# Turning the first chunk of the normed x at the layer change by VectorE blocks and DRAM

## The chip, the cores and the metric

The kernel runs on one core of one Trainium2 chip. The metric is the device time of one execution in microseconds (us). The time before is the median of three runs.

## The reference

Two layers of a decoder trunk over 512 tokens of width 1024. Each layer norms x, projects it once, feeds four groups of heads, gates them, projects back, norms again and adds to x:

```python
def hybrid_layer(x, mem, pre_g, post_g, w_in, ..., mem_norm_g, w_mem_kv, w_out):
    hn = rmsnorm(x, pre_g)
    proj = hn @ w_in                       # 1024 -> 6664 columns
    (ret_q, ..., xbc, z, dt_raw, sb_q, sb_k, sb_v, sb_g, mem_q, mem_g) = jnp.split(proj, ...)
    y_ret = retention(...) * silu(ret_g)
    y_ssd = ssd_mixer(xbc, z, dt_raw, ...)
    y_sb = stick_breaking(sb_q, sb_k, sb_v) * silu(sb_g)
    y_mem = memory_read(mem_q, rmsnorm(mem, mem_norm_g), w_mem_kv) * silu(mem_g)
    y = jnp.concatenate([y_ret, y_ssd, y_sb, y_mem], axis=-1) @ w_out
    return x + rmsnorm(y, post_g)          # x of the next layer
```

All is float32. What matters here is the seam between layer 0 and layer 1: `x + rmsnorm(y, post_g)`, then `rmsnorm(x, pre_g)` of the next layer, then the first products `hn @ w_in`, for which hn has to lie with its features on the partitions.

## The kernel before

The tokens are cut into four chunks of 128 (t = 0 to 3, `NT`). Matmuls in full precision are three products of two halves: `split` writes a high part (fp32r, a CAST on ScalarE, L293) and the remainder (a subtraction on VectorE, L294), and `mm3` (its matmuls all stand at L285) multiplies high by high, high by low and low by high. The normed x is kept turned, features first, as `hTh` (high) and `hTl` (low), each 128 partitions by 8 feature blocks by 512 tokens. Weights stream in through ScalarE's DMA queue (L353) as `raw`, and are split into `wh` and `wl` (five buffers each). PSUM has four banks named `pj` and four named `mx`. SBUF work tiles come from slots `s` (33), `y` (16) and `r` (9).

The layer change lies in `out_proj`. The second half of the output projection runs the four chunks two steps apart, so their sums end one after the other. For each chunk `post` then takes the square sums (ScalarE, L1168), a reciprocal root on GpSimd (L449 and L450), the new x on VectorE (L1170, two of L1172), two stores of it to DRAM for the end of layer 1 (SP's queue, L1179), the norm for layer 1 (two squares on ScalarE, L462; GpSimd again; two products on VectorE, L470, each 128x512), and turns the result. `turned` (through `prenorm`) turns 128x512 twice: four TensorE transposes of 128x128 into one `mx` bank (L479), then `split` from the bank into `hTh` and `hTl`.

While that goes on, TensorE does work of layer 1 that does not need x: the keys of the memory (`mem_k`, called twice, 256 columns wide) and its values (`mem_v`). `behind` ties the place of a transpose to these: the turn of chunk 0 stands behind the last matmul of the first `mem_k`, that of chunk 1 behind the second, that of chunk 2 behind a late matmul of `mem_v`, and that of chunk 3 (in `sb_v`) behind one in the first products with x. The first reader of `hTh` is `sb_v`'s `proj_a` (264 columns: 256 of a value block and 8 of the time steps); it runs chunk by chunk, chunk 0 first. Its banks are `pj` banks that `mem_k2` empties (VectorE, L570).

Apart from these ties, a scheduler with a model of time sets the order on each engine. Each engine then works strictly in that order, waiting on semaphores; SP's queue too.

The kernel already has another way to turn a tile, for the attention weights: VectorE's transpose turns each 32x32 block in place of the whole, four DMAs write the four groups of 32 partitions so that the blocks land in turned places of a DRAM tile, and one DMA reads the tile back (`through_dram`, L645 to L652: writes at L650, read at L651):

```python
        for a in range(P // BLK):
            self.nc.sync.dma_start(dst[a], v3(T[BLK * a:BLK * a + BLK], n))
        self.nc.sync.dma_start(out, src)
```

The functions that the diff touches:

Of the kernel before, what the change touches and what calls it, by code (L numbers as in the profile page):

```python
# [8 lines left out]
F32 = mybir.dt.float32  # L9
# [7 lines left out]
P = 128  # L17
SEQ = 512
NT = SEQ // P
D = 1024  # L20
KC = D // P
# [132 lines left out]

BLK = 32
TT = "y"
ST, SL, SB1, SB2 = "s", "y", 2, 4
# [11 lines left out]
def v3(ap, a):  # L171
    return ap.rearrange("p (a b) -> p a b", a=a)


class Builder:
# [305 lines left out]
            out(4 * i, b)  # L481
        return first

    def prenorm(self, x, gB, t):
        return self.turned(self.normed(x, gB), t)

    def turned(self, hn, t):
        ts = slice(P * t, P * t + P)
# [141 lines left out]
    def mem_turn(self, h, w, y):  # L630
        nc = self.nc
        pT = []
        for m in range(2):
            T = self.buf(tag="y")
            for i in range(2):
                x = w[i].rearrange("p (t m j b) -> p m t j b", t=2, m=2, b=BLK)[:, m]
                nc.vector.transpose(T.rearrange("p (j t b) -> p t j b", t=NT, b=BLK)[:, 2 * i:2 * i + 2], x)
            d = self.turned_rows(P, SEQ)
            dd = d.rearrange("(j m) (a t) -> a m j t", m=BLK, a=P // BLK)
            pT.append(self.through_dram(T, dd, d, self.buf(tag="y")))  # L640
# [5 lines left out]
    def through_dram(self, T, dst, src, out):  # L646

        n = dst.shape[2]
# [3 lines that stand above are left out]
        return out  # L652

    def columns_turned(self, tiles, out):
# [3 lines left out]
        for k, x in enumerate(tiles):  # L658
            T = self.buf(n, TT)
            self.nc.vector.transpose(T, x)  # L660
            dd = d[:, P * k:P * k + P].rearrange("(b t) (a f) -> a t b f", t=BLK, a=P // BLK)
            for a in range(P // BLK):
# [433 lines left out]
    def y_pair(self, kc):  # L1096
        return self.pair(self.yT[OUT_KEYS[kc]])

    def out_proj(self, l):
        nc = self.nc  # L1100
        last = l == DEPTH - 1
        y_pair, ys, ys2 = self.y_pair, self.ys, {}
        self.turn = []
        banks = [self.pj() for _ in range(NT)]
        for kc in range(16):
            if 1 <= kc < 15:
                ys[kc + 1] = y_pair(kc + 1)
            elif kc == 15:
                ys2 = {0: y_pair(0), 1: y_pair(1)}
            if kc % 2 == 0:  # L1110
                self.tick()
                w = self.w_take(2)
            for t in range(NT):
                self.out_unit(banks[t], ys[kc], kc, t, w)
            if kc % 2:
                self.w_prefetch()
            if kc == 6 and not last:
                self.mem_load()
            if kc == 8 and not last:
                self.mem_tiles()  # L1120
                for i in range(4):
                    self.mem_pairs(l + 1, i)
        postB = self.bcast_row(self.a["post_norm_g"][l:l + 1])
        preB = None if last else self.bcast_row(self.a["pre_norm_g"][l + 1:l + 2])
        y0 = [self.buf() for _ in range(NT)]
        ss = [self.tiny(2) for _ in range(NT)]
        for t in range(NT):
            nc.vector.tensor_tensor(out=y0[t], in0=banks[t], in1=postB[0], op=ALU.mult)
            nc.scalar.activation(banks[t], banks[t], AF.Square, scale=1.0 / 32.0, accum_out=ss[t][:, 0:1])
            self.with_eps(ss[t][:, 0:1])  # L1130
        banks = [self.mx() for _ in range(NT)]
        ys, subs, x1 = ys2, {}, []
        for step in range(16 + self.SKEW * (NT - 1)):
            if step == 8:
                xs = [self.load_x(t) for t in range(NT)]
            if 2 <= step + 1 < 16:
                ys[step + 1] = y_pair(step + 1)
            for t in range(NT):
                kc = step - self.SKEW * t
                if not 0 <= kc < 16:  # L1140
                    continue
                if kc // 2 not in subs:
                    subs[kc // 2] = self.w_take(2)
                self.out_unit(banks[t], ys[kc], kc, t, subs[kc // 2])
                if t == NT - 1 and kc % 2:
                    self.w_prefetch()
                if kc == 15:
                    x1.append(self.post(l, t, xs[t], y0[t], banks[t], ss[t], postB[1], preB))
        self.yT = {}
        self.xsrc = x1  # L1150
        if not last:
            for i in range(2):
                self.mem_k2(self.mem_k(i))
                self.behind(self.turn[i], self.last_mm)
            self.mem_v()
            self.behind(self.turn[2], self.marks[5])

    def load_x(self, t):
        x = [self.buf(), self.buf()]
# [4 lines left out]
    def post(self, l, t, x, y0, bank, ss, g1, preB):  # L1164

        nc = self.nc
        y1, junk = self.buf(), self.buf()
        nc.scalar.activation(junk, bank, AF.Square, scale=1.0 / 32.0, accum_out=ss[:, 1:2])  # L1168
        r = self.rstd(ss[:, 0:1], ss[:, 1:2])
        nc.vector.tensor_tensor(out=y1, in0=bank, in1=g1, op=ALU.mult)  # L1170
        for i, y in enumerate((y0, y1)):
            nc.vector.scalar_tensor_tensor(out=x[i], in0=y, scalar=r, in1=x[i], op0=ALU.mult, op1=ALU.add)  # L1172
        if preB:
            d = self.dr.tile([P, D], F32, tag="x1", name=self.name("x1"), bufs=NT)[:]
            self.turn.append(self.prenorm(x, preB, t))
        else:
            d = self.a["out"][P * t:P * t + P]
        for i in range(2):
            nc.sync.dma_start(d[:, 512 * i:512 * i + 512], x[i])  # L1179
        return d  # L1180
# [154 lines left out]
```

## Time and profile before

| | |
|---|---|
| median of 3 runs | 922.68 us (922.54 to 923.47) |
| profiled execution | 923.25 us, its span 921.5 us |
| granted TensorE clock over the span | 0.998 |
| busy: TensorE, VectorE, ScalarE, GpSimd | 99%, 73%, 48%, 16% of the span |
| layer change (first L1168 to first reads of hTh) | 461 to 488 us of the span |

The span is what the profiler saw from the first to the last instruction; 1.75 us of the execution lie around it. Places in the span are given in us from its start. In a row of the timeline, the first number is the start, the second the length of the merged piece, and a bracket at the end tells idle time before it and what ended that. TensorE's matmuls overlap in such rows, so the distance from one start to the next, not the length, is what one of them takes. PE is TensorE, PEld its weight load, DVE VectorE, ACT ScalarE, POOL GpSimd, SP the queue of SyncE; a q behind the name is the engine's instruction queue.

### The profile page before, as it was taken

The page shows a single profiled execution, that of the slowest core. Times are in us where ns is not written, and L with a number is a line of the kernel's source. Part 1 is how long each engine was busy: PE and PEld are TensorE (multiplying, and loading weights), DVE is VectorE, ACT ScalarE, POOL GpSimd, SP SyncE. Part 2 cuts the span into 40 slices and gives each one's busy share as a digit, 9 for nine tenths or more (in the row PEclk, how much of TensorE's full clock was granted, in tenths as well). Part 3 has the DMA queues.
Part 4 walks back from the last instruction along what each step waited for, and adds up shares of the span by engine and source line. Part 5 has one row for each costly group of instructions (what it writes and reads, how often), then busy time and mean ns, then how long its engine had stood idle before and what let it go on. Part 6 is the DMA issues. An engine that isn't in the chain of part 4 may idle for free.

```text
span 921.5 us, 12952 instructions
## 1 busy us (share of the span) xinstructions
PE 913.2 (99%) x4667; PEld 773.6 (84%) x4667; DVE 673.3 (73%) x1081; ACT 443.5 (48%) x841; POOL 146.3 (16%) x208
## 2 busy tenths in 40 slices
PE   9999999999999999999999999999999999999997
PEld 7998888888888888888899888888888888888885
DVE  6855689888787887844587476898778869687343
ACT  6643485744453342733465336675445434335341
POOL 1200152320131110100040002423112120102001
PEclk9999999999999999999999999999999999999999
DMA  8544664642444333444345256556333362422502
GB/s 316 213 141 144 169 167 104 199 146 61 120 134 148 116 109 126 137 149 158 116 173 196 93 172 183 124 122 183 103 109 116 110 194 92 139 95 88 210 12 91
DMA packets 105408, 128.53 MB, mean 139 GB/s; under 512 B 64640, under 2 KB 79744, under 8 KB 96256
## 3 DMA queue, kind: packets, MB, share of 16 engines
q10 hardware_dynamic: 10224, 73.44, 23.4%
q1 hardware_dynamic: 95120, 54.28, 20.7%
q8 instruction: 36, 0.59, 0.3%
q14 instruction: 28, 0.23, 0.1%
HBM read 112.10 MB, written 15.56 MB: 139 GB/s over the span
## 4 chain that ended last, share of the span: by engine, by line
PE 98%; DMA 1%; ACT 0%; DVEq 0%; SPq 0%; POOLq 0%; issue 0%; POOL 0%; ACTq 0%; DVE 0%
PE pj L285 74%; PE mx L285 23%; PE mx L479 1%; DMA mem<-memT 1%; PE mx L1003 0%; ACT s L523 0%; DVEq L1331 0%; ACT s L1168 0%; POOLq L1331 0%; ACT wh L293 0%; SPq L506 0%; SPq L349 0%; SPq L1206 0%; POOL t L449 0%; ACTq L1331 0%
## 5 line engine op out<-in xcount | busy, mean ns | idle before, releaser
L285 PE MATMUL pj<-hTh,wh 128*128 128x512 f32 x704 | 276.4, 393 | 0.0
L285 PE MATMUL pj<-hTh,wl 128*128 128x512 f32 x704 | 275.8, 392 | 0.0
L285 PE MATMUL pj<-hTl,wh 128*128 128x512 f32 x704 | 274.6, 390 | 0.0
L294 DVE TENSOR_TENSOR wl<-raw,wh 128x1024 fp32r<-128x1024 f32 (+2 forms) x156 | 188.6, 1214 | 116.9 <-ACT wh L293 115.7
L293 ACT CAST wh<-raw 128x1024 fp32r<-128x1024 f32 (+2 forms) x156 | 158.7, 1020 | 205.0 <-PE pj L285 177.5
L285 PEld LDWEIGHTS pj<-hTh,wl 128*128 128x128 f32 x704 | 132.2, 188 | 27.3
L285 PEld LDWEIGHTS pj<-hTh,wh 128*128 128x128 f32 x704 | 132.3, 188 | 27.1 <-DVE s L593 0.8
L285 PEld LDWEIGHTS pj<-hTl,wh 128*128 128x128 f32 x704 | 132.3, 188 | 26.6
L285 PE MATMUL pj<-wh,s 128*128 128x512 f32 x320 | 97.6, 391 | 0.0
L285 PE MATMUL mx<-s,s 128*128 128x256 f32 (+4 forms) x528 | 79.7, 307 | 0.0
L285 PE MATMUL mx<-wh,s 128*128 128x512 f32 x256 | 79.2, 389 | 0.0
L285 PEld LDWEIGHTS mx<-s,s 128*128 128x128 f32 (+1 forms) x528 | 65.8, 177 | 8.2 <-PE pj L285 1.4
L285 PEld LDWEIGHTS pj<-wh,s 128*128 128x128 f32 x320 | 59.7, 188 | 12.4
L285 PE MATMUL pj<-wl,s 128*128 128x512 f32 x160 | 60.2, 389 | 0.0
L285 PEld LDWEIGHTS mx<-wh,s 128*128 128x128 f32 x256 | 48.1, 188 | 10.0
L294 DVE TENSOR_TENSOR s<-y,s 128x512 fp32r<-128x512 f32 x64 | 41.2, 687 | 19.7 <-ACT s L293 14.0
L262 ACT ACTIVATE s<-s 128x128 f32<-128x128 f32 (+3 forms) x96 | 41.8, 478 | 22.3 <-DVE s L733 20.6
L675 POOL TENSOR_TENSOR s<-y,s 128x512 fp32r<-128x512 f32 x16 | 23.7, 1494 | 179.9 <-ACT s L674 179.4
L293 ACT CAST s<-y 128x512 fp32r<-128x512 f32 x64 | 36.6, 617 | 30.8 <-PE mx L285 22.0
L285 PE MATMUL mx<-wl,s 128*128 128x512 f32 x128 | 49.6, 389 | 0.0
L285 PE MATMUL pj<-wl,hTh 128*128 128x256 f32 (+2 forms) x144 | 47.6, 331 | 0.0
L285 PE MATMUL pj<-wh,hTl 128*128 128x256 f32 (+2 forms) x144 | 47.5, 330 | 0.0
(185 smaller groups left out, 1298.5 us busy)
## 6 DMA issues: line engine op xcount, KB each, us to landing
raw<-wts ACTq DMA_DIRECT2D x69, 1024.0 KB, 4.8
s<-x SPq DMA_DIRECT2D x24, 256.0 KB, 4.1
y<-turned SPq DMA_DIRECT2D x24, 256.0 KB, 2.8
turned<-y SPq DMA_DIRECT2D x64, 64.0 KB, 2.2
s<-acs SPq DMA_DIRECT2D x16, 256.0 KB, 6.3
r<-row SPq DMA_DIRECT2D x12, 256.0 KB, 5.0
raw<-wts SPq DMA_DIRECT2D x4, 512.0 KB, 7.5
raw<-wts SPq DMA_DIRECT2D x2, 1024.0 KB, 6.3
```

The source lines that it names most:

```text
L262: i = self.nc.scalar.activation(out, in_, func, **k)
L285: return self.nc.tensor.matmul(out, lhsT, rhs, start=start, stop=stop)
L293: self.nc.scalar.copy(h, src)
L294: self.nc.vector.tensor_sub(l, src, hf)
L479: x = self.nc.tensor.transpose(b[:, P * j:P * j + P], hn[i][:, P * j:P * j + P], self.con("ident", P))
L675: nc.gpsimd.tensor_sub(p.l, x, p.hf)
```

## The change

For chunk 0 alone (`FAR` = 1) the eight TensorE transposes go. Each of the two 128x512 halves of the normed x is turned by one VectorE transpose into a `y` slot, written to a DRAM tile of 512x128 by four DMAs of 64 KB (runs of 128 bytes), read back by one DMA of 256 KB (runs of 512 bytes) into another `y` slot, and split from there. Chunks 1 to 3 are turned as before. The tie of chunk 0's transposes to `mem_k` goes with them; the other ties stay.

```diff
+LT, LL, FAR = "y", "y", 1
...
-    def prenorm(self, x, gB, t):
-        return self.turned(self.normed(x, gB), t)
+    def turned_far(self, hn, t):
+        ts = slice(P * t, P * t + P)
+        H, HF, L = v3(self.hTh[:], KC), v3(self.hTh[:].bitcast(F32), KC), v3(self.hTl[:], KC)
+        for i in range(2):
+            T, ks = self.buf(tag=LT), slice(4 * i, 4 * i + 4)
+            self.nc.vector.transpose(T, hn[i])
+            d = self.turned_rows(SEQ, P)
+            dd = d.rearrange("(b m) (a t) -> a m b t", m=BLK, a=P // BLK)
+            x = self.through_dram(T, dd, d.rearrange("(k p) t -> p k t", p=P), v3(self.buf(tag=LL), 4))
+            self.split(x, H[:, ks, ts], L[:, ks, ts], HF[:, ks, ts])
...
                 self.mem_k2(self.mem_k(i))
-                self.behind(self.turn[i], self.last_mm)
+                if i >= FAR:
+                    self.behind(self.turn[i], self.last_mm)
...
-            self.turn.append(self.prenorm(x, preB, t))
+            self.turn.append((self.turned_far if t < FAR else self.turned)(self.normed(x, preB), t))
```

The scheduler orders the seam anew. GpSimd's order is the same as before, and on the other engines nothing changes outside the layer change and the first few projections of layer 1. In the rows below a name carries a running number, which differs between the two programs; after the change a line stands 1 to 12 lines further down (L479 is L480, L470 is L471, L1172 is L1184, L293 and L294 are L294 and L295).

VectorE at the norm of chunk 0 and what follows it. Before: s_4544 and s_4545 are the normed halves of chunk 1, hTl from mx_4492 and mx_4499 is chunk 0, s_4332 and s_4333 are the new x of chunk 2.

```order
L294 TENSOR_TENSOR wl_4694<-raw_4376,wh_4693 128x1024
L294 TENSOR_TENSOR wl_4724<-raw_4450,wh_4723 128x1024
L1170 TENSOR_TENSOR s_4585<-mx_4214,s_4185 128x512
L470 SCALAR_TENSOR_TENSOR s_4544<-s_4328,t_4549,s_4188 128x512
L470 SCALAR_TENSOR_TENSOR s_4545<-s_4329,t_4549,s_4189 128x512
L294 TENSOR_TENSOR hTl<-mx_4492,hTh 128x4x128
L1172 SCALAR_TENSOR_TENSOR s_4332<-s_4194,t_4588,s_4332 128x512
L294 TENSOR_TENSOR hTl<-mx_4499,hTh 128x4x128
L1172 SCALAR_TENSOR_TENSOR s_4333<-s_4585,t_4588,s_4333 128x512
L294 TENSOR_TENSOR wl_4759<-raw_4450,wh_4758 128x1024
L294 TENSOR_TENSOR wl_4789<-raw_4697,wh_4788 128x528
```

The same place after (y_4492 and y_4503 are the block-turned halves of chunk 0, y_4495 the first half read back):

```order
L295 TENSOR_TENSOR wl_4702<-raw_4376,wh_4701 128x1024
L491 STREAM_TRANSPOSE y_4492<-s_4482 128x512
L295 TENSOR_TENSOR wl_4732<-raw_4450,wh_4731 128x1024
L1182 TENSOR_TENSOR s_4593<-mx_4214,s_4185 128x512
L471 SCALAR_TENSOR_TENSOR s_4552<-s_4328,t_4557,s_4188 128x512
L471 SCALAR_TENSOR_TENSOR s_4553<-s_4329,t_4557,s_4189 128x512
L1184 SCALAR_TENSOR_TENSOR s_4332<-s_4194,t_4596,s_4332 128x512
L295 TENSOR_TENSOR wl_4767<-raw_4450,wh_4766 128x1024
L1184 SCALAR_TENSOR_TENSOR s_4333<-s_4593,t_4596,s_4333 128x512
L295 TENSOR_TENSOR wl_4797<-raw_4705,wh_4796 128x528
L491 STREAM_TRANSPOSE y_4503<-s_4483 128x512
L295 TENSOR_TENSOR hTl<-y_4495,hTh 128x4x128
```

One transpose stands behind the first of two weight splits, the other eight instructions later; chunk 0's first low half moves from ahead of chunk 2's new x to behind it, and its second low half, 12 rows further on, stands just ahead of chunk 3's norm.

ScalarE between the squares of chunk 2 and the third block of 264 columns' weights. Before (s_4596 and s_4597 are the squares of chunk 2, s_4632 the square sum of chunk 3, hTh from mx_4554 and mx_4561 is chunk 1):

```order
L293 CAST wh_4788<-raw_4697 128x528
L462 ACTIVATE s_4596,t_4595<-s_4332 128x512
L462 ACTIVATE s_4597,t_4595<-s_4333 128x512
L1168 ACTIVATE s_4632,t_4199<-mx_4215 128x512
L293 CAST hTh<-mx_4554 128x4x128
L353 DMA raw_4762<-wts 128x1056
L293 CAST hTh<-mx_4561 128x4x128
L293 CAST wh_4848<-raw_4697 128x528
L462 ACTIVATE s_4642,t_4641<-s_4336 128x512
L462 ACTIVATE s_4643,t_4641<-s_4337 128x512
L293 CAST wh_4854<-raw_4762 128x528
```

After (hTh from y_4495 and y_4506 are the two halves of chunk 0 as they come back from DRAM):

```order
L463 ACTIVATE s_4604,t_4603<-s_4332 128x512
L354 DMA raw_4770<-wts 128x1056
L294 CAST hTh<-y_4495 128x4x128
L463 ACTIVATE s_4605,t_4603<-s_4333 128x512
L1180 ACTIVATE s_4640,t_4199<-mx_4215 128x512
L294 CAST hTh<-mx_4562 128x4x128
L294 CAST hTh<-mx_4569 128x4x128
L294 CAST wh_4856<-raw_4705 128x528
L463 ACTIVATE s_4650,t_4649<-s_4336 128x512
L294 CAST wh_4862<-raw_4770 128x528
L463 ACTIVATE s_4651,t_4649<-s_4337 128x512
L294 CAST hTh<-y_4506 128x4x128
```

The cast of the first half now stands between the two squares of chunk 2, that of the second behind the squares of chunk 3.

TensorE at the first reads of hTh. Before, pj_4877 (chunk 0) takes twelve matmuls, and then pj_4878 (chunk 1):

```order
L285 MATMUL pj_4877<-wh_4848,hTh 128x264
L285 MATMUL pj_4877<-wl_4849,hTh 128x264
L285 MATMUL pj_4877<-wh_4848,hTl 128x264
L285 MATMUL pj_4878<-wh_4788,hTh 128x264
L285 MATMUL pj_4878<-wl_4789,hTh 128x264
```

After, with pj_4885 for chunk 0, pj_4886 for chunk 1 and wh_4862 the first weights of the second half of the features:

```order
L286 MATMUL pj_4885<-wl_4857,hTh 128x264
L286 MATMUL pj_4885<-wh_4856,hTl 128x264
L286 MATMUL pj_4885<-wh_4862,hTh 128x264
L286 MATMUL pj_4886<-wh_4796,hTh 128x264
L286 MATMUL pj_4886<-wl_4797,hTh 128x264
```

Chunk 0's first half of features is read by the 1st matmul of this block as before, the second half's high part by the 13th, and its low part by the 27th. Before, chunk 0's transposes stood as two groups of four in the second `mem_k`; there is nothing in their place now, and chunk 1's two groups of four have become one of eight, 20 matmuls into `mem_v`.

SP's queue gets ten DMAs: four writes and a read behind the two stores of chunk 1's x, and four writes and a read behind the two stores of chunk 2's x. The stores of chunk 3's x stand behind all of these.

More of the change, by code (lines that the diff above doesn't have):

```diff
@@ L1153, in out_proj @@
                 self.mem_k2(self.mem_k(i))
-                self.behind(self.turn[i], self.last_mm)
+                if i >= FAR:
+                    self.behind(self.turn[i], self.last_mm)
             self.mem_v()
-            self.behind(self.turn[2], self.marks[5])
+            if FAR < 3:
+                self.behind(self.turn[2], self.marks[5])
     def load_x(self, t):
```

## The prediction

> **What bounds the kernel now.** First the busy times and the chain that ended last, from the page, and the waits of TensorE over the whole run.
>
> ```profile
> PE 913.2 (99%) x4667; PEld 773.6 (84%) x4667; DVE 673.3 (73%) x1081; ACT 443.5 (48%) x841; POOL 146.3 (16%) x208
> PE 98%; DMA 1%; ACT 0%; DVEq 0%; SPq 0%; POOLq 0%; issue 0%; POOL 0%; ACTq 0%; DVE 0%
> PE mx L285 <- POOL b L197: 1.2, 1, 1.2
> PE pj L285 <- ACT s L523: 1.0, 2, 0.7
> ```
>
> TensorE is busy for all but 8 us, the chain is TensorE for 98%, and its only two waits belong to the start (L197 is the warm-up, L523 the first memory tiles). From then on it never waits, so what is taken off it comes off the end, as long as no new wait appears. Next the seam itself, engine by engine (columns: length, PE, PEld, DVE, ACT, POOL busy with counts, granted clock, DMA share, GB/s).
>
> ```profile
> 455.00:475.00 20.00, 20.00 (x139) 18.61 (x138) 15.75 (x20) 11.72 (x23) 6.84 (x12) 1.00 0.53 186
> 475.00:488.00 13.00, 13.00 (x68) 10.85 (x68) 12.56 (x20) 8.95 (x21) 4.92 (x8) 1.00 0.51 185
> 488.00:515.00 27.00, 27.00 (x216) 26.38 (x215) 16.75 (x33) 11.74 (x21) 0.00 (x0) 1.00 0.47 165
> ```
>
> TensorE is full and at full clock in all three. VectorE is busy for 12.56 of 13 us from 475 to 488: it sits off the chain with almost no room, so any work added there has to be followed to its reader.
>
> **The term that counts: eight transposes less.** The chain around them (start and length), then rows of TensorE's timeline:
>
> ```profile
> 470.41 0.44 PE mx L479 x4
> 470.85 0.24 PE pj L285 x2
> 471.08 0.44 PE mx L479 x4
> ...
> 475.19 0.40 PE L285 MATMUL pj<-wh,s 128*128 128x512 f32 x1
> 487.96 0.28 PE L285 MATMUL pj<-wh,hTh 128*128 128x264 f32 x1
> 488.08 0.28 PE L285 MATMUL pj<-wl,hTh 128*128 128x264 f32 x1
> 490.88 1.04 PE L479 MATMUL mx<-consts,s 128*128 128x128 f32 x8
> ```
>
> The two groups of chunk 0 take 0.44 each, 0.88 us on the path. The two matmuls between them keep their 0.12 each. Chunk 1's two groups become one of eight and chunk 3's eight become two groups of four; neither counts, since the chain shows a group of four at 0.44 and I take eight as two of these. Everything behind moves 0.88 us up: `mem_v` begins at 474.31 instead of 475.19, the first read of hTh comes at 487.08 instead of 487.96. Its matmuls follow each other by 0.12 (487.96 to 488.08), so the 13th, which needs the second half of chunk 0, starts at 488.5, the 27th, which needs its low part, at 490.2, and chunk 3's transposes, after the 31st, at 490.8.
>
> **What replaces them, and its cover.** VectorE, now (timeline), and by groups of one shape the mean of one in ns:
>
> ```profile
> 469.52 2.35 DVE L294 TENSOR_TENSOR wl<-raw,wh 128x1024 fp32r<-128x1024 f32 x2
> 471.79 0.68 DVE L1170 TENSOR_TENSOR s<-mx,s 128x512 f32<-128x512 f32 x1
> 472.91 1.42 DVE L470 SCALAR_TENSOR_TENSOR s<-s,t,s 128x512 f32<-128x512 f32 x2 [0.44 <-POOL t L450]
> 474.24 0.68 DVE L294 TENSOR_TENSOR hTl<-mx,hTh 128x512 fp32r<-128x512 f32 x1
> 474.84 0.74 DVE L1172 SCALAR_TENSOR_TENSOR s<-s,t,s 128x512 f32<-128x512 f32 x1
> 476.76 1.84 DVE L294 TENSOR_TENSOR wl<-raw,wh 128x1024 fp32r<-128x1024 f32 x2
> 479.64 1.41 DVE L470 SCALAR_TENSOR_TENSOR s<-s,t,s 128x512 f32<-128x512 f32 x2 [0.44 <-POOL t L450]
> 484.11 1.28 DVE L570 TENSOR_TENSOR s<-pj,mrow 128x512 f32<-128x512 f32 x2
> L745 DVE STREAM_TRANSPOSE s<-s 128x512 f32<-128x512 f32 x8 | 5.5, 689 | 3.3 <-POOL s L736 3.3
> L294 DVE TENSOR_TENSOR hTl<-mx,hTh 128x512 fp32r<-128x512 f32 x16 | 10.4, 684 | 1.9 <-ACT hTh L293 1.9
> L293 ACT CAST hTh<-mx 128x512 fp32r<-128x512 f32 x16 | 8.7, 587 | 6.2 <-PE mx L479 6.1
> L293 ACT CAST s<-y 128x512 fp32r<-128x512 f32 x64 | 36.6, 617 | 30.8 <-PE mx L285 22.0 <-DVE y L1075 8.6
> ```
>
> A 128x512 block transpose takes 0.69, pipelined about 0.6, as an hTl subtraction of 0.68 does (474.24 to 474.84). The first starts when the first of the two wl splits ends, at 470.7, and ends at 471.4. It pushes what follows by 0.6, of which the idle 0.44 before L470 takes most. Then the two hTl of chunk 0 are missing (1.2 us), so the second transpose ends at about 478.1. The two hTl return later and the two casts on ScalarE cost 0.62 instead of 0.59, nothing. VectorE has 1.2 us more to do in all.
>
> The round trip, from rows of the same path in the first heads of layer 0 (SP's queue), what DMAs take to land, and the busy times of that stretch:
>
> ```profile
> 78.94 1.77 SPq L650 DMA_DIRECT2D turned<-y  x4
> 82.20 0.34 SPq L651 DMA_DIRECT2D y<-turned  x1
> ...
> 94.48 1.74 SPq L650 DMA_DIRECT2D turned<-y  x4
> 101.17 0.34 SPq L651 DMA_DIRECT2D y<-turned  x1
> ...
> y<-turned SPq DMA_DIRECT2D x24, 256.0 KB, 2.8
> turned<-s SPq DMA_DIRECT2D x32, 64.0 KB, 2.0
> DMA to landing us min/median/max: 1.4/2.4/7.8
> ...
> 60.00:200.00 140.00, 140.00 (x662) 117.34 (x662) 105.38 (x195) 78.03 (x176) 32.32 (x36) 1.00 0.53 146
> ```
>
> From the first write's issue to the read's issue 3.26 us (78.94 to 82.20), then 2.8 to land: 6.1. The slowest of these starts took 6.69 (94.48 to 101.17): 9.5. With the longest landing for the read as well, 6.69 + 7.8 = 14.5. The writes of the new path have 64 KB in the shape of the row that lands in 2.0. I take 6.1: its start lies in the stretch of the last row, whose DMA share of 0.53 is that of the seam (0.51 to 0.53). 9.5 and 14.5 stay for the range.
>
> First half: 471.4 + 6.1 = 477.5 in SBUF, cast by 478.1, subtracted by 478.7, against a first read at 487.08. Second half: 478.1 + 6.1 = 484.2, cast by 484.9 (behind chunk 3's squares), against 488.5; its subtraction stands behind a wl split on VectorE, done by 486.7, against 490.2. Both are hidden under `mem_v`.
>
> What queues behind the new waits matters more, since each engine works in order. ScalarE now has the first half's cast between chunk 2's two squares:
>
> ```profile
> 476.88 0.63 ACT L462 ACTIVATE s<-s 128x512 f32<-128x512 f32 x1 [0.35 <-DVE s L1172]
> 482.05 0.63 ACT L293 CAST wh<-raw 128x528 fp32r<-128x528 f32 x1 [1.73 <-PE pj L285]
> ```
>
> The second square ran at 476.88; behind a cast that ends at 478.1 it is 1.2 late, and with it the square sum of chunk 3, GpSimd's two roots, and VectorE's norm of chunk 2, which ran at 479.64 and now starts at about 479.9. Half of ScalarE's delay is eaten before 482.05, where it idled 1.73 for TensorE anyway. L570, which empties the `pj` bank of the first hTh product, started at 484.11 and now at 484.3: its first half is done by 484.9, against 487.08. That is 2.2 us of room, the smallest I find. Chunk 3's norm ends at about 488.0 (behind the second half's subtraction), against 490.8: 2.8.
>
> SP's queue: the stores of chunk 2's and 3's x stand behind reads that wait for their writes, some 3 us each; they are read back at the end of layer 1, 400 us later. ScalarE's load of the second 528 KB of weights moves ahead of the cast, the 1 MB load after it falls back about 1 us; nothing else is moved past a queue. The two `y` slots per half and the two `mx` banks saved change no reader: `y` tiles of layer 0 are consumed before the norm.
>
> So the sum is -0.88 + 0 = -0.88 us. Against its own time, the profiled execution of 923.25 (span 921.5 and 1.75 around it) gives 922.37; the median of the runs is 0.57 below that execution, so 922.68 - 0.88 = 921.80. That is 0.095%, below the 0.2% (1.85 us) that a measurement of this kernel can tell from no change.
>
> **A rule on headroom.** The row has 84% for PEld beside 99% for PE. The Trainium skill, Perfetto Trace Analysis, section Identifying the Most-Contended Engine, calls matmul busy time no good measure of headroom and names the busy share of the weight loads instead. By it TensorE would have 16% to spare and taking work off it might bring nothing, 922.68. No row of a wait after the start supports that here, so it becomes a rival with a small chance.
>
> **Rivals.**
>
> *The gain does not show.* TensorE's rows fill the span by modelled ends; if the two matmul streams on each side were paced by the weight loads, the eight transposes could lie in their slack. For it: PEld busy 10.85 of 13 us from 475 to 488. Against it: those transposes hold 0.44 per group between two matmuls 0.12 apart. Time 922.7. Chance 0.08.
>
> *ScalarE holds the seam, a little.* The trip of the first half takes 9.5 instead of 6.1 (a 528 KB weight load starts at the same moment). The cast, chunk 2's second square, the norm on VectorE and L570 all move by the same 3.4; with 2.2 us of room TensorE waits 1.2 for the bank of its first hTh product. Net +0.3: 923.0. For it: the start at 94.48 shows such a trip. Against it: the start at 78.94 took 3.3, at the same mean DMA share. Chance 0.18.
>
> *ScalarE holds the seam, and the kernel is slower.* The same mechanism; it decides from a trip of 6.1 + 2.2 + 0.88 + 1.85 = 11.0 us on. At the bound of 14.5 the wait is 6.2 and the time 922.68 - 0.88 + 6.2 = 928.0. Against it: no row of the path reaches 11.0, only the longest landing added to the slowest start does. Chance 0.07. The Trainium skill, VectorE: DVE Perf Modes, section Rules for kernel authors, advises TensorE for a 128x128 transpose whenever PSUM will do as its target, which speaks for this side; the rows speak against it only because TensorE is the full engine here.
>
> *Faster than 0.2%.* It would need 1 us more off TensorE, and no wait is there to be removed; only the new order of matmuls between 488 and 515 could do it. About 920.5. Chance 0.03.
>
> **How the numbers follow.** The forecast, no stall and -0.88, has 0.64. Within 0.2% lie the forecast, the gain that does not show and the small stall: 0.64 + 0.08 + 0.18 = 0.90, of which I give 0.02 to a small stall that grows past the bound. So same 0.88, slower 0.09, faster 0.03. The range runs from 921.2 (the runs scatter by half a microsecond) to 923.4, the small stall with the same scatter; outside stay the slow tail and the fast one.
>
> **What would show it.** Right: 56 transposes in place of 64 on TensorE; no wait of TensorE behind the start; the first hTh product about 0.9 earlier; two block transposes of 128x512 near 470.7 and 477.5 at 0.69; a wait of ScalarE for the read near 477 of about 1 us, and VectorE's L570 (now L580) at about 484.3. Wrong: a wait of TensorE at the first `pj` product with hTh (released by VectorE) or at its 13th (by ScalarE), or transposes of chunk 2 or 3 that wait for VectorE. The prediction fails if the round trip at this place is over 8.3 us, or if a group of transposes is worth much more or less than 0.44.

## The result and the profile after

The changed kernel takes 926.06 us (median of 7 runs, 924.97 to 927.33), the kernel before 923.16 us (7 runs beside them, 922.54 to 923.58): a ratio of 1.0032, 95% interval 1.0022 to 1.0041. It is 2.9 us slower, where 0.9 us less was forecast. The profiled execution took 927.25 us with a span of 925.5, 4.0 more than the span of before.

First the waits of TensorE after the change, over the whole run (engine, bank, line, what it waited for; total us, times, longest):

```profile
PE pj L286 <- DVE s L580: 2.5, 1, 2.5
PE mx L286 <- POOL b L198: 1.2, 1, 1.2
PE pj L286 <- ACT s L533: 1.0, 2, 0.7
```

The last two are those of the start, as before. The first is new, and is the wait that the prediction named under "wrong": the first product with hTh waits for VectorE's L580 (L570 before), which empties its bank. The same stretches of the seam as before (length, PE, PEld, DVE, ACT, POOL busy, granted clock, DMA share, GB/s):

```profile
455.00:475.00 20.00, 20.00 (x135) 18.48 (x135) 16.14 (x20) 11.12 (x23) 6.73 (x12) 1.00 0.62 196
475.00:488.00 13.00, 12.72 (x63) 10.00 (x61) 7.68 (x12) 4.88 (x12) 1.69 (x5) 1.00 0.59 146
488.00:515.00 27.00, 24.80 (x194) 24.83 (x195) 20.95 (x39) 15.33 (x30) 0.98 (x3) 0.94 0.49 176
```

Two things to see. VectorE and ScalarE, busy 12.56 and 8.95 us from 475 to 488 before, are busy 7.68 and 4.88: they stand and wait there, and their work moves into the next stretch. And the clock of the last stretch is 0.94.

Now TensorE's rows. The first is a matmul ahead of the seam that both programs have (457.59 in the kernel before, shown first), then the first matmul of `mem_v` and the first product with hTh after the change:

```profile
457.59 0.28 PE L285 MATMUL pj<-s,wl 128*128 128x256 f32 x1
```
```profile
457.78 0.28 PE L286 MATMUL pj<-s,wl 128*128 128x256 f32 x1
...
474.52 0.40 PE L286 MATMUL pj<-wh,s 128*128 128x512 f32 x1
...
485.70 1.32 PE L480 MATMUL mx<-consts,s 128*128 128x128 f32 x8
...
490.20 0.36 PE L286 MATMUL pj<-wh,hTh 128*128 128x264 f32 x1 [2.47 <-DVE s L580]
...
492.57 0.42 PE L286 MATMUL pj<-wh,hTl 128*128 128x264 f32 x1
492.79 0.42 PE L286 MATMUL pj<-wh,hTh 128*128 128x264 f32 x1
```

From that matmul to `mem_v` it is 475.19 - 457.59 = 17.60 before and 474.52 - 457.78 = 16.74 after: the eight transposes gave 0.86. From it to the first hTh product it is 487.96 - 457.59 = 30.37 before and 32.42 after, 2.05 more in spite of that. From there to the end of the span it is 921.5 - 487.96 = 433.5 before and 925.5 - 490.20 = 435.3 after, another 1.8. With 0.2 from the start of the run these are the 4.0. The last two rows show where most of the 1.8 comes from: the products follow each other by 0.22 there (492.57 to 492.79), by 0.12 before. The second run of this kernel (a1_again below) puts this part at 1.5; the other 0.3 is not worked out.

The wait is followed back along the chain of waits from 455 to 515 (start, length):

```profile
473.04 3.30 DMA turned<-y
476.47 5.95 DMA y<-turned
482.45 0.04 ACT hTh L294
...
482.97 0.73 ACT s L463 x2
...
484.11 0.57 POOL t L451
...
484.90 0.92 DVE s L471 x2
...
489.38 0.68 DVE s L580
...
490.20 5.54 PE pj L286 x31
```

The chain reads: the writes to DRAM land, the read takes 5.95 us, ScalarE's cast of the first half, the second square of chunk 2 behind it, GpSimd's root, VectorE's norm of chunk 2 and what stands behind that, L580, TensorE. This is the mechanism of the two rivals in which ScalarE holds the seam. The queues around the read (SP's, then ScalarE's timeline):

```profile
471.58 2.10 SPq L660 DMA_DIRECT2D turned<-y  x4
476.47 0.39 SPq L661 DMA_DIRECT2D y<-turned  x1
```
```profile
476.42 0.38 ACTq L354 DMA_DIRECT2D raw<-wts  x1
482.45 0.62 ACT L294 CAST hTh<-y 128x512 fp32r<-128x512 f32 x1 [6.28 <-DMA y<-turned]
482.97 0.63 ACT L463 ACTIVATE s<-s 128x512 f32<-128x512 f32 x1
```

From the first write's issue to the read's issue it is 4.89, and the read lands 5.95 later, at 482.42: a trip of 10.8 us in place of 6.1. ScalarE's load of 528 KB of weights leaves at 476.42, 0.05 ahead of the read. The two squares of chunk 2 are the L463 rows; the first ran at 475.45, ahead of the cast, the second behind it. These rows gave the theory for the experiments: the load leaving in the same moment makes the read slow; the cast, in order ahead of the second square, makes the slow read a wait; and the granted clock, which falls 1.3 us after the wait has ended (the products are about 0.12 apart until 491.50), makes it dearer.

### The profile page after: what moved, and what is told of

It reads as the page before. It is cut to its first block, busy times and chain, and to the rows that moved or that the text cites. A ratio compares the mean times of both kernels' runs of the same rounds, so it can differ in the third digit from the quotient of the medians.

```text
span 925.5 us, 12954 instructions
## 1 busy us (share of the span) xinstructions
PE 914.6 (99%) x4659; PEld 774.5 (84%) x4659; DVE 673.8 (73%) x1083; ACT 442.8 (48%) x841; POOL 144.1 (16%) x208
## 4 chain that ended last, share of the span: by engine, by line
PE 95%; DMA 2%; DVE 1%; ACT 1%; issue 0%; SPq 0%; DVEq 0%; POOL 0%; POOLq 0%; ACTq 0%
PE pj L286 72%; PE mx L286 23%; DMA y<-turned 1%; DMA mem<-memT 1%; PE mx L480 0%; PE mx L1013 0%; DMA turned<-y 0%; DVE s L1184 0%; DVE s L471 0%; ACT s L463 0%; ACT wh L294 0%; ACT s L533 0%; SPq L660 0%; DVEq L1343 0%; DVE hTl L295 0%
## 5 line engine op out<-in xcount | busy, mean ns | idle before, releaser
L295 DVE TENSOR_TENSOR wl<-raw,wh 128x1024 fp32r<-128x1024 f32 (+2 forms) x156 | 188.3, 1212 | 118.3 <-ACT wh L294 117.2
L294 ACT CAST wh<-raw 128x1024 fp32r<-128x1024 f32 (+2 forms) x156 | 158.4, 1021 | 209.2 <-PE pj L286 184.5
L295 DVE TENSOR_TENSOR s<-y,s 128x512 fp32r<-128x512 f32 x64 | 41.2, 686 | 19.7 <-ACT s L294 14.0
L294 ACT CAST s<-y 128x512 fp32r<-128x512 f32 x64 | 36.5, 617 | 29.3 <-PE mx L286 22.0
L286 PE MATMUL pj<-wh,hTh 128*128 128x256 f32 (+2 forms) x144 | 48.0, 337 | 2.5 <-DVE s L580 2.5
```

The source lines that it names most:

```text
L286: return self.nc.tensor.matmul(out, lhsT, rhs, start=start, stop=stop)
L294: self.nc.scalar.copy(h, src)
L295: self.nc.vector.tensor_sub(l, src, hf)
```

## The experiments

Each kernel ran on the same chip beside the kernel before, and each ratio is to that one's runs there. In the diffs `far` holds the cast and the subtraction of each half of chunk 0, `sq` the squares of the norms (two a chunk), `nrm` the norm's products, `k2` the two instructions of L570, `xn` the halves of the new x, `wl[k]` the weight splits on VectorE, `ld5` the 528 KB load. `behind(a, b)` places a behind b. Line numbers shift: L580 is L587 or L593 in some, the casts L501.

**e1_trip: the trip without its reader.** TensorE turns chunk 0 as before; the transposes on VectorE, the writes and the reads are done as well, and nobody uses what comes back.

```diff
             x = self.through_dram(T, dd, ..., v3(self.buf(tag=LL), 4))
-            self.split(x, H[:, ks, ts], L[:, ks, ts], HF[:, ks, ts])
+        return self.turned(hn, t)
```

> Before, plus the round trip of chunk 0 alone (two block transposes, eight writes, two reads); nobody reads what comes back, TensorE still turns chunk 0. Theory A (the loss is ScalarE and VectorE standing in order behind a cast that waits for the trip): nothing waits for the trip, so no wait of TensorE, 922.7 to 923.7, the same as before. Theory B (the trip's DMAs and the 1.3 us of VectorE delay the weights or the other chunks): TensorE waits as in the changed kernel, 925 or more.

Measured 923.46 against 922.90, ratio 1.0007 (0.9998 to 1.0016). No wait at the first hTh product, so the writes, the reads and VectorE's 1.4 us of transposes don't make the wait of 2.5 by themselves. The test is not the whole of it: chunk 0's subtractions are back on VectorE, so the 528 KB load left 1.00 behind the first read, and that read landed in 2.9. And the traffic is not free. A 1 MB weight load that left 0.92 behind the second read took 8.5 us to land, ScalarE waited 4.42 for it, and TensorE 0.8 at 495.4 for a cast behind that.

**e2_late: the casts stand later.** All of the change stays; the cast of the first half stands behind the squares of chunk 3, and the subtractions behind L587 and behind the norm of chunk 3.

```diff
+            self.behind(self.far[0][0], self.sq[7])
+            self.behind(self.far[0][1], self.k2[1])
+            self.behind(self.far[1][1], self.nrm[7])
```

> The change, with chunk 0's first cast placed behind chunk 3's squares on ScalarE, its first subtraction behind the two products that empty the banks of the keys, and its second behind chunk 3's norm; the trip itself is left alone. Theory A: the wait of 2.5 us before the first product with hTh goes, what is left is at most a short wait for the second half (it came back at about 489.5, its first reader stands at about 490): 921.8 to 923.3. Theory C (the halves are simply back too late for TensorE, in whatever order): TensorE waits 2 us or more at a product that reads chunk 0, 924 or more.

Measured 922.94 against 922.90, ratio 0.9997 (0.9988 to 1.0005), and the wait is gone. Rows of SP's queue, ScalarE, the DMA view of 474 to 478 (KB, us to landing), and VectorE:

```profile
475.69 0.38 SPq L670 DMA_DIRECT2D y<-turned  x1
```
```profile
475.86 0.34 ACTq L354 DMA_DIRECT2D raw<-wts  x1
...
483.68 0.60 ACT L501 CAST hTh<-y 128x512 fp32r<-128x512 f32 x1
```
```profile
y<-turned SPq DMA_DIRECT2D x1, 256.0 KB, 5.3
```
```profile
483.19 1.28 DVE L587 TENSOR_TENSOR s<-pj,mrow 128x512 f32<-128x512 f32 x2
```

The read is slow here too, 5.3 us, with the load 0.17 behind it. But the cast stands where it finds its data, nothing is queued behind a wait, and L587 runs at 483.19 in place of 489.38. So the slow read cost nothing here, where nothing had to wait behind its reader.

**e3_noload: the load stands behind the cast.**

```diff
+            self.behind(self.ld5, self.far[0][0])
```

> The change, with the second 528 KB load of weights issued behind the cast of chunk 0's first half instead of ahead of it; in the changed kernel it was issued at 476.42 and the read of the first half at 476.47. If this load is what made the read take 6.0 us to land: the read lands in 3 to 4, the cast starts at about 480 instead of 482.45, TensorE's wait falls from 2.5 to under 0.5, 922 to 923. If it is not (the stores of x, or the read itself): the read still takes 6, and the time stays at 925 to 927.

Measured 923.36 against 922.90, ratio 1.0001 (0.9992 to 1.0010). The cast keeps its place between the squares, but the read, issued at 477.88 here (this execution waited 1.1 us more than that of before at its start), lands in 2.9 in place of 5.95:

```profile
480.76 0.62 ACT L501 CAST hTh<-y 128x512 fp32r<-128x512 f32 x1 [3.19 <-DMA y<-turned]
480.77 0.35 ACTq L354 DMA_DIRECT2D raw<-wts  x1
```

No wait at the first hTh product; one of 0.3 for a cast of chunk 3, at 497.0. TensorE's order, up to the first hTh product and 26 products beyond, is that of the changed kernel. So the load beside the read was what made it slow, and either half of the theory, taken away alone, takes the loss away.

**e4_first: the first half alone goes through DRAM**, TensorE turns the second. I expected the loss to stay, since the first half's cast stands as it did.

```diff
         for i in range(2):
+            if i != HALF:        # HALF = 0
+                ... four transposes on TensorE, split from the bank
+                continue
             T, ks = self.buf(tag=LT), slice(4 * i, 4 * i + 4)
```

> Half of the change: only the first 128x512 half of chunk 0 goes by VectorE and DRAM, the second is turned by TensorE. The cast of the half that comes back still stands between chunk 2's squares. Theory A: the wait is the first half's, so it stays at 1.5 to 2.5 us while only 0.44 is saved: 924.2 to 925.5, and 2 more where the clock falls. If it is the second half's trip that costs: no wait, 922.7.

That was wrong: 922.28 against 922.90, ratio 0.9998 (0.9989 to 1.0006), no wait. The reason is in two rows, SP's and ScalarE's:

```profile
476.60 0.39 SPq L670 DMA_DIRECT2D y<-turned  x1
```
```profile
477.33 0.33 ACTq L354 DMA_DIRECT2D raw<-wts  x1
479.62 0.62 ACT L294 CAST hTh<-y 128x512 fp32r<-128x512 f32 x1 [2.70 <-DMA y<-turned]
```

The load left 0.73 behind the read, and the read landed in 3.0. The load waits for the weight split on VectorE that frees its buffer; in this kernel one subtraction of hTl (0.68) is back ahead of that split, so the split ends later. (In every trace here but that of e3_noload, where it is tied to the cast, the load leaves 0.03 behind that split's end.) The outcome is also the one that I had put down to the second half's trip, but with the first read this quick the run can't tell. So the next three kernels move the load against the read, with both halves through DRAM (e5_swap, e6_ahead) and with the first alone (e7_ahead1).

**e5_swap: two VectorE instructions exchanged.** The changed kernel, with the weight split that frees the load's buffer behind the second half of chunk 2's x. The other ties hold the rest near the order that it had: up to the first hTh product ScalarE's cast of one weight half moves one place, and three products of TensorE pass the transposes of chunk 2; behind it more is ordered anew.

```diff
+            self.behind(self.wl[2 * NBLK + 7], self.xn[5])
+            self.behind(self.far[0][0], self.ld5)
+            self.behind(self.sq[5], self.far[0][0])
+            self.behind(self.wl[2 * NBLK + 10], self.k2[1])
```

> The changed kernel with two VectorE instructions in exchanged order: the wl split that releases ScalarE's 528 KB load, and the half of chunk 2's x behind it. The load then leaves 0.6 us behind the read in place of 0.05 ahead. Theory (the load ahead of the read makes the loss): read lands in about 3 us, cast at 479.5, L587 at about 486 in place of 489.4, no wait of TensorE, 922.0 to 923.0. Rival (the place of the cast between chunk 2's squares, or the order of the matmuls, makes it): as the changed kernel, 925 to 927.3.

Measured 923.38 against 923.19, ratio 1.0004 (0.9996 to 1.0013): the loss of the changed kernel, 1.0030 beside the same runs, is gone, with the cast still between the squares.

```profile
476.67 0.38 SPq L670 DMA_DIRECT2D y<-turned  x1
```
```profile
477.55 0.33 ACTq L354 DMA_DIRECT2D raw<-wts  x1
479.65 0.62 ACT L501 CAST hTh<-y 128x512 fp32r<-128x512 f32 x1 [3.17 <-DMA y<-turned]
```
```profile
486.57 1.28 DVE L587 TENSOR_TENSOR s<-pj,mrow 128x512 f32<-128x512 f32 x2
```

The load leaves 0.88 behind the read, which lands in 3.0. From the read's issue L587 comes after 9.9 us, in the changed kernel after 12.9. The median is 0.4 above what I expected: a wait of 0.5 for another bank (VectorE, L612) has appeared. (The profiled execution, 924.28, also waited 1.0 longer at its start.) So both halves can go through DRAM with the cast between the squares, if the load leaves behind the read.

**e6_ahead: late casts, and the load well ahead of the read.**

```diff
+            (the three lines of e2_late)
+            self.behind(self.xn[4], self.wl[2 * NBLK + 7])
+            self.behind(self.sq[4], self.ld5)
```

> The late casts of e2_late, and ScalarE's 528 KB load made to leave about 0.5 us ahead of the first half's read (VectorE's wl split that releases it stands one place earlier, and the load ahead of chunk 2's first square). Theory (a late read costs only what is queued behind its cast): the read lands 5 to 6 us after its issue, at about 482, nobody stands behind it, L587 at 483 to 485, no wait of TensorE: 922.0 to 923.3. Rival (a read behind the load costs in itself, or the late casts had only luck with the order of read and load): 924.5 to 927.3.

Measured 922.36 against 923.19, ratio 0.9993 (0.9984 to 1.0002), no wait behind the start. The load left at 475.42, 0.46 ahead of the read at 475.88, and the read took 4.5, less than the 5 to 6 that I expected; L587 at 483.42. First hTh product:

```profile
457.45 0.28 PE L286 MATMUL pj<-s,wl 128*128 128x256 f32 x1
...
486.90 0.28 PE L286 MATMUL pj<-wh,hTh 128*128 128x264 f32 x1
```

From the matmul ahead of the seam it takes 29.45, against 30.37 before: 0.92 less.

**e7_ahead1: one half as e4_first, the load well ahead of the read** (the two lines of e6_ahead without the late casts, and the second half's subtraction behind the same split).

> The first half alone through DRAM, as e4_first, with the 528 KB load made to leave about 0.5 us ahead of its read in place of 0.7 behind. Theory (the load ahead of the read makes the loss): the read lands in 5 to 6 us in place of 3.0, cast at 481.8 to 482.6, L593 at 488.5 to 489.5 against a first hTh product due at about 487.7; TensorE waits 1 to 2 us, 923.5 to 926.5. Rival (one half alone is harmless wherever the load stands): 922.3.

Measured 923.47 against 923.19, ratio 1.0001 (0.9992 to 1.0010). TensorE waits again at the first hTh product, which it did not in e4_first, but less than expected:

```profile
475.44 4.48 DMA y<-turned
```
```profile
487.70 0.36 PE L286 MATMUL pj<-wh,hTh 128*128 128x264 f32 x1 [0.63 <-DVE s L593]
```

The load left 0.43 ahead (475.01); the read took 4.5, not 5 to 6, and the wait is 0.6, not 1 to 2. The direction of the theory holds, its size did not: a load with a lead of 0.4 is worse than one 0.7 behind, and better than one in the same moment. One half alone is not harmless wherever the load stands, so e4_first was no proof against the first half.

**a1_again: the changed kernel once more**, to see why its times lie at 925 and at 927.

> The changed kernel once more, unchanged. Its seven times lay at 925.0 to 925.5 (mean clock 0.999) and at 927.2 to 927.3 (0.996). Theory (the clock makes the second step): TensorE waits 2 to 2.5 us at its first hTh product in every execution, and in some of them its granted clock then falls. A profile near 925.3 shows the wait, the read of the first half landing in about 6 us behind ScalarE's 528 KB load, and a clock of 1.00 from 488 to 515; one near 927.2 shows 0.94 there. Rival (the race makes the second step): near 925.3 the read left ahead of the load, landed in about 3 us, and TensorE waits at most 0.5.

Measured 925.89 against 923.19 (924.95 to 928.1, 6 runs), ratio 1.0030 (1.0019 to 1.0042). The profiled execution is one of the lower ones, 925.37 us, span 923.6:

```profile
476.32 5.75 DMA y<-turned
```
```profile
489.83 0.36 PE L286 MATMUL pj<-wh,hTh 128*128 128x264 f32 x1 [2.47 <-DVE s L580]
490.03 0.28 PE L286 MATMUL pj<-wl,hTh 128*128 128x264 f32 x1
490.15 0.28 PE L286 MATMUL pj<-wh,hTl 128*128 128x264 f32 x1
```

The read is as slow and the wait is the same 2.47, to the hundredth. What differs stands in the windows from 491 to 495, of the first profile of the changed kernel and of this one:

```profile
491.00:495.00 4.00, 4.00 (x23) 4.00 (x22) 4.00 (x8) 2.77 (x7) 0.00 (x0) 0.57 0.61 244
```
```profile
491.00:495.00 4.00, 4.00 (x36) 4.00 (x35) 4.00 (x7) 3.07 (x6) 0.00 (x0) 1.00 0.56 231
```

23 matmuls at a granted clock of 0.57 against 36 at 1.00. From the first hTh product to chunk 3's first transposes it is 495.57 - 490.20 = 5.37 in the one and 493.68 - 489.83 = 3.85 in the other: 1.5 us. So both profiled executions pay the wait, and one of the two paid the clock as well. That the clock's fall is the wait's doing is argued: no other wait lies near it, but no run takes the one away and leaves the other.

How often the clock falls here isn't shown, and I had read too much into the mean clocks. The times don't fall into two groups: one of the first seven lay at 926.06 with a clock of 0.998, and here there are 925.72 with 0.997, 926.06 and 926.42 with 0.998. A mean of 0.996 doesn't say where the clock fell either: the profiled execution of e3_noload has it with 1.00 from 488 to 515, and 0.51 from 11.0 to 14.5, behind a wait of 1.8 that ended at 8.67, in its start.

The Trainium skill, TensorE: Matmul & The Clock Gate, Part 1 (the HAM clock gate), has the array at half rate after an idle window of about 3.4 us, and the window running free, so that the same kernel meets it differently from run to run. The half rate and the chance agree with these rows; the length does not bind as stated, since 2.47 us of waiting were enough, if it was the wait that did it.

**b1_best and b2_both: versions that keep the gain.** b1_best is e6_ahead again; b2_both joins the late casts of e2_late to the exchange of e5_swap.

> e6_ahead once more, unchanged, as the version that keeps the eight transposes off TensorE without the wait. Theory (the term of 0.88 us is real and nothing else is lost): 0.7 to 1.0 us below the kernel before of the same call, no wait of TensorE behind the start, the first hTh product at about 487.1 where the span has no extra wait at its start. Rival (the gain does not show, the transposes lay in slack): within 0.3 us of the kernel before.

> The late casts of e2_late and the exchanged order of e5_swap together, so that the 528 KB load leaves 0.7 us or more behind the first half's read. Theory: the read lands in about 3 us, nobody waits, as b1_best: 0.7 to 1.0 us below the kernel before of the same call. Rival (the gain does not show): within 0.3 us of it.

b1_best took 922.93 against 923.43, ratio 0.9996 (0.9987 to 1.0005). With e6_ahead the same kernel was 0.8 and 0.5 below the kernel before; in the trace its first hTh product again stands 29.45 behind the matmul ahead of the seam. In time the gain is not shown, since both intervals hold 1; in the trace it is, up to that product. Behind it b1_best has a wait that I hadn't expected, at a product with chunk 3:

```profile
496.10 0.39 PE L286 MATMUL mx<-wh,hTh 128*128 128x264 f32 x1 [0.36 <-ACT hTh L294]
```

ScalarE had stood 2.91 us for the 1 MB weight load, which landed in 6.5 here and in 5.4 in e6_ahead, and the cast of chunk 3 stood behind that. From the matmul ahead of the seam to the end of the span, e6_ahead took 0.75 less than the kernel before, b1_best 0.15 less.

b2_both took 924.60 against 923.43, ratio 1.0015 (1.0006 to 1.0024), and is a miss. Its first read landed in 3.0 as expected, with the 528 KB load 0.59 behind it. But the scheduler put ScalarE's next load, 1 MB, ahead of the second half's cast (ScalarE's queue), and the second read left 0.77 behind it (the DMA view of 483 to 486):

```profile
483.98 0.33 ACTq L354 DMA_DIRECT2D raw<-wts  x1
490.99 0.62 ACT L501 CAST hTh<-y 128x512 fp32r<-128x512 f32 x1 [6.38 <-DMA y<-turned]
```
```profile
raw<-wts ACTq DMA_DIRECT2D x1, 1024.0 KB, 5.4
y<-turned SPq DMA_DIRECT2D x1, 256.0 KB, 6.2
```
```profile
PE mx L286 <- ACT hTh L294: 0.7, 1, 0.7
PE pj L286 <- ACT hTh L501: 0.2, 1, 0.2
```

The second read took 6.2, TensorE waited 0.2 for that cast at a product with the second half and 0.7 later for a cast that stood behind it. It is the same collision at the other half.

## Why the prediction was wrong, point by point

- **The gain of 0.88 on TensorE: right.** 0.86 by the start of `mem_v`, 56 transposes in place of 64, and 0.92 at the first hTh product of e6_ahead. With that, the rival that the gain does not show has fallen in the trace.
- **VectorE's transposes: right.** They ran at 470.85 and 477.58 with 0.71 each, against 470.7 and 477.5 with 0.69.
- **The trip of 6.1: this step failed.** It was 10.8. Both parts were too short. Writes to read took 4.9, not 3.26: for the first half it was 4.6 to 5.0 in every kernel run here, so the row at 78.94 was a good case. That alone would have given 7.4 to 7.8 with a read of 2.8, still within the 8.3 that I named. The landing of 5.95, not 2.8, broke it. I had chosen by the mean DMA share of two stretches, 0.53 in both. A mean over 140 us doesn't tell what leaves in the same moment. The order rows told it. The two hTl subtractions of chunk 0 leave their place ahead of the weight split on VectorE (1.2 us), and one half of chunk 2's new x goes behind that split (0.7); 0.3 of this goes to a later start and the transpose. So the split starts at 475.17 in place of 476.76, its buffer comes free earlier, and the load leaves at 476.42 in place of 478.01, where ScalarE's timeline had it before:

```profile
478.01 0.33 ACTq L353 DMA_DIRECT2D raw<-wts  x1
```
```profile
475.17 1.22 DVE L295 TENSOR_TENSOR wl<-raw,wh 128x1024 fp32r<-128x1024 f32 x1
```

  It took both: e5_swap takes back only the second and e4_first one of the subtractions, and in each the load leaves behind the read again. I noted the load among what moves and priced it at nothing, but for the chance of the second rival.
- **The second half: wrong as well.** It was to be in SBUF at 484.2; its read was issued at 485.40, behind writes that took until then, and its cast ran at 489.38. Nobody waited for it, because TensorE was already late by then. b2_both shows that there was little room.
- **The room of 2.2 at L570: right.** The trip was 4.7 longer than taken, less 2.2 of room makes 2.5; the wait is 2.47. That it fits to the hundredth is luck: L580 ran 5.1 later than forecast, not 4.7, and TensorE was later too. The mechanism was that of the second and third rival, at 10.8 between their 9.5 and 14.5.
- **The price of the wait: too small.** By the sum of the rivals a trip of 10.8 gives -0.9 + 2.5 = +1.6 us, and the third rival was to decide only from 11.0 on. Measured were 2.1 more span in the execution without the clock's fall and 4.0 in the one with it. Missing were the clock, 1.5, and smaller pieces that aren't listed among TensorE's waits. The product behind the wait starts 2.88 us after the one ahead of it (487.32 to 490.20), where the kernel before has 0.23 (487.73 to 487.96): it comes 2.65 late, not 2.47, since matmuls that follow each other overlap in these rows and those on both sides of a wait don't. And the transposes of chunk 2, which now stand behind the late norm, took 0.3 more (485.70, with 1.32 in place of 1.03), though only 0.1 more in a1_again. The rest, up to 0.3 behind the first hTh product, stays open.

So the chances were wrong where they leaned on one number: with the read's slow case tied to an event that was visible in the order, the rivals that took 0.25 together were the likely ones.

## What to carry to other kernels

When an edit takes work off an engine, look for the transfers which that engine releases: here two subtractions that went, and one instruction that changed places, let a weight load go 1.6 us earlier, into the moment of the read that the edit had added. A reader of a DRAM round trip belongs where its data surely is there, and not ahead of work that somebody waits for; moved behind chunk 3's squares, a read nearly as slow (5.3 us) cost nothing. And a wait of a full TensorE is priced with its aftermath, not by its length alone: here a wait of 2.5 us was followed by 1.5 more of a fallen clock in one of two profiled executions.

## What the runs showed of the hardware

How long a 256 KB read on SP's queue takes beside a 528 KB load on ScalarE's depends on their distance in time by tenths of a microsecond:

| kernel | load's issue, from the read's | read lands in | load lands in |
|---|---|---|---|
| b1_best, e6_ahead, e7_ahead1 | 0.58, 0.46, 0.43 ahead | 4.4, 4.5, 4.5 | 3.9, 4.1, 4.0 |
| changed kernel, a1_again | 0.05, 0.03 ahead | 5.95, 5.75 | 5.4, 5.1 |
| e2_late | 0.17 behind | 5.3 | 5.0 |
| b2_both, e4_first, e5_swap, e1_trip | 0.59, 0.73, 0.88, 1.00 behind | 3.0, 3.0, 3.0, 2.9 | 5.1, 5.2, 5.7, 6.0 |
| e3_noload | 2.89 behind | 2.9 | 4.7 |

Each row but the second is one execution a kernel, and two 256 KB stores of x leave 0.5 to 0.8 behind every one of these reads. The one that leaves clearly first is the quicker for it; leaving together, the read is slower than in either other case, and the load about as slow as when it leaves behind. The Trainium skill, DMA: Bandwidth & Descriptors, Queues, rings and completion order, has each DMA engine take turns between the queues that have work for it, packet by packet; that two transfers which leave together both take longer than one that leaves clearly first agrees with it. Why a distance of half a microsecond matters so much isn't shown by any run here.

A row for the granted clock was also new to me: it fell to 0.57 over 4 us after a wait of 2.47 in one execution, and stayed at 1.00 after the same wait in another. The wait of 0.63 in e7_ahead1 was followed by a clock of 1.00 in its profile. At the start of the execution, waits of 1.7 in e4_first and e5_swap were followed by 1.00, one of 1.8 in e3_noload by 0.51.
